# A gated-attention layer's projections in K blocks of 4, 5 and 7 tiles instead of 8 and 8

## The chip, the cores and the metric

The kernel runs on one core of a Trainium2 chip. The core's engines work through queues of their own: the matrix engine (PE, with its weight loads PEld), VectorE (DVE), ScalarE (ACT), GpSimd (POOL) and SyncE (SP), which issues nearly all transfers from HBM. PE writes to PSUM banks, from which DVE and ACT read. An instruction waits at the head of its engine's queue until what it needs is there, and everything behind it waits too. The metric is the device time of one execution in microseconds; the median of several executions is given.

## The reference

A trunk of two layers on 256 tokens of width 2048, all in float32. Layer 0 mixes tokens by gated linear attention (GLA), layer 1 by forgetting attention (FoX); each is followed by a gated MLP with a short convolution. Every sub-layer gets a normalised and modulated input, and the modulation comes from a vector c through a large matrix.

```python
cond = jax.nn.silu(c)
for i in range(DEPTH):
    mod = (cond @ w_mod[i] + b_mod[i])[:, None, :]
    sh_m, sc_m, g_m, sh_f, sc_f, g_f = jnp.split(mod, 6, axis=-1)
    h = rmsnorm(x, norm_mix[i]) * (1.0 + sc_m) + sh_m
    ...
    x = x + (1.0 + g_m) * y          # y: GLA or FoX of h
    h = rmsnorm(x, norm_ffn[i]) * (1.0 + sc_f) + sh_f
    x = x + (1.0 + g_f) * conv_ffn(h, ...)

def gla_mixer(h, w_in, w_gate, b_gate, g_norm, w_out):
    q, k, v, r, a = jnp.split(h @ w_in, ...)   # 1024, 1024, 2048, 2048, 16 columns
    log_alpha = log_sigmoid(a @ w_gate + b_gate) / 16
    ...
```

Only the first part of layer 0 is touched: the columns of sh_m and sc_m (2048 each, a sum over 2048 rows of w_mod), h, and the product h @ w_in.

## The kernel before, in words

Every product is done in three passes, since PE rounds its operands: an operand is split into a rounded part and the rest, and high times high, low times high and high times low are added in PSUM. For the weights, ACT casts a tile of 128 rows by 1024 columns (wh, L120) and DVE subtracts (wl, L124). For the input, `make_h` (L498) works tile by tile of K: DVE multiplies x by the inverse root (hn, L517), ACT applies scale and shift with rounding (h, L518), DVE does it again without rounding (L519) and subtracts (L520). In PE's rows L602 is high times high, L603 the input's low part, L604 the weight's low part; L638 to L640 are the same for v, where h is the moving operand's partner; L652 to L654 the narrow product a. In the changed kernel these lines are L615 to L617, L651 to L653 (v) and L665 to L667 (narrow), the splits L125 and L129, and make_h is L527 (DVE), L528 (ACT), L530 or L532 (new, on ACT) and L533 (DVE).

The projection h @ w_in is cut into seven pieces: q, k, v0, v1, r0, r1 (1024 columns each) and a (16). `gla` (L686) runs them in K blocks: q, k, v0 on K tiles 0 to 3, the same three on tiles 4 to 7, then a, v1, r0, r1 on tiles 0 to 7; `gla_rest` (L732) runs all on tiles 8 to 15. The reason for blocks is that h of a K tile needs its 128 columns of sc_m and sh_m, and these sums take time. `fold` (L702) takes a finished piece out of its four banks: the first part by ACT (L713), later ones by additions on DVE (L715).

The modulation columns come in two ways. The first 512 of each are summed on PE (`early_sum`, L1246: c times 4 tiles of w_mod; then a copy on ACT, L1252, and four narrow products, L1255). The others are accumulated on DVE in the background (`mod_tasks`, L266 and L268, one 128-row tile at a time; then a 32x32 transpose, L278, a reduction, L279, and one product with a constant, L295, before DVE adds the bias, L311). Before, sc_m of tiles 4 to 7 went that way and sh_m of tiles 4 to 7 on PE, in `finish_late` (L1286).

The order of the work is set by the order in which the program is written, with small priorities, and the queues keep it. `tick` (L356), called behind each K tile of a piece, takes a step of the background list when a pace counter is full; `set_pace` spreads the list over so many ticks, and `drain_bg` empties it. The last three tiles of a piece are held and run bank by bank (TAIL), so that banks come free one after another; they have no tick. `split_to` (L561) keeps the splits three tiles ahead of PE and the loads up to six ahead of the splits. The gate's chain in `gla_rest` (products with w_gate L745, log-sigmoid on ACT and DVE L680 to L683, cumulative products L764) is a second list, paced by pace["side"].

Of the kernel before, what the change touches and what calls it, by code (L numbers as in the profile page):

```python
# [13 lines left out]
AF = mybir.ActivationFunctionType  # L14
# [21 lines left out]
SLOAD = 12  # L36
BACK = 1
STAGE = 3
FREE = 0
PEND = 3  # L40
BLOCKS = (8, 8)
HEAD = 4
HEADED = ('q', 'k', 'v0')
# [10 lines left out]
GP0 = 0.7  # L54
# [3 lines left out]
N0, N5 = 4, 5  # L58
BG0, BG1 = 0.95, 0.45
# [13 lines left out]
def kernel(  # L73
# [20 lines left out]
    order = {"v": None, "t": None}  # L94
# [20 lines left out]
    def split_w(src, moving, after=None):  # L115
# [4 lines left out]
        nc.scalar.copy(out=hi, in_=src)  # L120
# [71 lines left out]
    nc.vector.tensor_scalar_mul(vec[:, r0["qn"]:r0["qn"] + 1], vec[:, r0["qn"]:r0["qn"] + 1], float(P) ** -0.5)  # L192
# [5 lines left out]
    def load_bmod():  # L198
        for hh in range(2):
            br = ringt([P, P], "brow")  # L200
            nc.scalar.dma_start(out=br[:96, :], in_=b_mod[hh].rearrange("(r p) -> r p", p=P))
            pb = misc()
            nc.tensor.transpose(pb[:, :96], br[:96, :], ident[:96, :96])
            nc.vector.tensor_copy(out=bm[:, hh * 96:(hh + 1) * 96], in_=pb[:, :96])
# [28 lines left out]
    startup = {"loads": [], "left": SLOAD}  # L233

    def after_startup(on=True):
        es = ExitStack()
        if on and startup["left"] > 0 and len(startup["loads"]) >= BACK:
            startup["left"] -= 1
            es.enter_context(tc.issue_after(startup["loads"][-BACK]))
        return es  # L240

    def mod_tasks(l, key, f0=0, fn=D, wide=False, defer=False, turn=False):
# [8 lines left out]
        def chunk(c0, kt, st):  # L251
            def load():
                st[kt] = bigt([P, per, width], "wm") if wide else ringt([P, per, width], "wm")
                src = w_mod[l, kt * P:(kt + per) * P, s * D + c0:s * D + c0 + width]
                with after_startup():
                    nc.sync.dma_start(out=st[kt], in_=src.rearrange("(k p) m -> p k m", p=P))
# [99 lines left out]
    def tick():  # L356
        prefetch(PEND)
        flush_resting()
        with ExitStack() as es:
# [3 lines left out]
            steps()  # L363

# [133 lines left out]
    def make_h(l, kind):  # L498
# [12 lines left out]
        def make(m):  # L511
# [7 lines left out]
            nc.vector.tensor_scalar(out=t, in0=t, scalar1=sc, scalar2=sh, op0=ALU.mult, op1=ALU.add)  # L519
# [31 lines left out]
    def next_w(kt, cols, hold=None):  # L551
# [4 lines left out]
        if i < STAGE:  # L556
            run, look = min(run, STAGE - i), 1
        split_to(min(i + 1 + run, len(plan)), look)
        return splits.popleft()

    def split_to(end, look=LOOK):  # L561
        while fetched["split"] < end:
            while fetched["load"] < min(fetched["split"] + look, len(plan)):
# [4 lines left out]
                for c0, cn in cols_:  # L568
                    if nk_ == 1:
                        with after_startup():  # L570
                            nc.sync.dma_start(out=wt[:, o:o + cn], in_=w_[kt_ * P:(kt_ + 1) * P, c0:c0 + cn])
                        o += cn
                    else:
                        nc.sync.dma_start(out=wt[:, :nk_ * cn].rearrange("p (k r) -> p k r", r=cn),
                                          in_=w_[kt_ * P:(kt_ + nk_) * P, c0:c0 + cn]
                                          .rearrange("(k p) r -> p k r", p=P))
# [109 lines left out]
    def gla(l, h, finish_late):  # L686
# [35 lines left out]

        run(HEADED, ALL[:HEAD])
        drain_bg()
        finish_late()
        run(HEADED, ALL[HEAD:BLOCKS[0]])
        run([key for key, _ in pieces if key not in HEADED], ALL[:BLOCKS[0]])
        drain_bg()
        kts = ALL[BLOCKS[0]:]
        return kts, pieces, piece, fold, parts  # L730

    def gla_rest(l, kts, pieces, piece, fold, parts):  # L732
# [3 lines left out]
        nc.sync.dma_start(out=wg[RANK:RANK + 1, :], in_=gla_b_gate)  # L736
        fold("a", piece("a", kts, off["a"]))
# [46 lines left out]
        pace["side"], pace["sacc"] = 1.0, 0.0  # L784

        fold("q", piece("q", kts, off["q"]))
# [21 lines left out]
        pace["side"] = 0.5  # L808
        fold("k", piece("k", kts, off["k"]))
# [573 lines left out]
```

## Time and profile before

| | us |
|---|---|
| median of 3 runs (lowest to highest) | 2430.47 (2429.18 to 2430.49) |
| the profiled execution | 2429.0 |
| its span, first to last instruction | 2427.0 |
| PE busy in it | 2384.6 |
| first full-width weight product with low weights (L604) | at 47.02 |
| idle of PE in front of the block boundary's first product (L652, at 192.41) | 1.86 |

The page counts an engine as busy while an instruction of it runs, and PE's count says nothing of the clock: a matmul of 256 columns starts 0.113 us behind the one before it at full clock and 0.213 us at half clock. So the idle rows and the granted clock are read together. All times are from the start of the span.

### The profile page before, as it was taken

Reading aid. Unit: us, or ns where it says so; the run is one execution under the profiler, and the core shown is the slowest. Engines: PE = TensorE matmul, PEld = TensorE weight load, DVE = VectorE, ACT = ScalarE, POOL = GpSimd, SP = SyncE. Lnnn points to the kernel's source line nnn. Section 1 sums busy time; section 2 is a strip of 40 time slices with the busy share of each in tenths; the row PEclk is TensorE's granted clock in tenths of the full one; section 3 lists DMA queues with packets and bytes.
Section 4 is the critical chain, followed back from the end, with each engine's and each line's share of the span. In section 5 each row is a group of like instructions: output and inputs, shape, how many; then the busy total and the mean of one; then the engine's idle time right before and its main releaser. Section 6 shows DMA issues by size and latency. Waiting matters only on the chain.

```text
span 2427.0 us, 46850 instructions
## 1 busy us (share of the span) xinstructions
PE 2384.6 (98%) x19127; PEld 2285.0 (94%) x19131; DVE 1922.6 (79%) x2609; ACT 1252.4 (52%) x1671; POOL 16.2 (1%) x35
## 2 busy tenths in 40 slices
PE   6999999899999999999999999999999999999998
PEld 4898899899999999999988889999999999999998
DVE  4898989888789999986687998877776767777544
ACT  4447454445556665543454455545555555565433
POOL 0000000000000000000000000000000000000000
PEclk9999999999999999999999999999999999999999
DMA  9986968898668988998589887686777777756552
GB/s 376 374 303 222 328 223 312 297 343 293 195 200 297 318 305 311 326 315 314 164 298 314 299 272 251 215 296 228 235 235 228 240 227 236 232 195 217 191 191 104
DMA packets 188148, 638.31 MB, mean 263 GB/s; under 512 B 23705, under 2 KB 24715, under 8 KB 187548
## 3 DMA queue, kind: packets, MB, share of 16 engines
q1 hardware_dynamic: 186968, 634.12, 76.9%
q8 instruction: 149, 2.44, 0.4%
q10 hardware_dynamic: 964, 1.20, 0.1%
q14 instruction: 67, 0.55, 0.1%
HBM read 633.14 MB, written 2.10 MB: 262 GB/s over the span
## 4 chain that ended last, share of the span: by engine, by line
PE 95%; DVE 3%; DMA 1%; ACT 1%; issue 1%; DVEq 0%; SPq 0%
PE pa L604 25%; PE pa L603 25%; PE pa L602 25%; PE pa L640 5%; PE pa L639 5%; PE pa L638 5%; DMA wm<-in_w_mod_dram 1%; DVE wl L124 1%; PE pe L1246 0%; PE pm L473 0%; DVE acc L268 0%; PE pm L846 0%; PE pm L868 0%; PE pm L1057 0%; PE pt L288 0%
## 5 line engine op out<-in xcount | busy, mean ns | idle before, releaser
L120 ACT CAST wh<-w 128x1024 fp32r<-128x1024 f32 x819 | 856.4, 1049 | 1001.8 <-PE pa L603 707.9
L124 DVE TENSOR_TENSOR wl<-w,wh 128x1024 fp32r<-128x1024 f32 x819 | 995.8, 1218 | 408.8 <-ACT wh L120 403.6
L603 PE MATMUL pa<-h,wh 128*128 128x256 f32 x3584 | 990.8, 278 | 3.9 <-DVE h L520 3.9
L602 PE MATMUL pa<-h,wh 128*128 128x256 f32 x3584 | 987.7, 278 | 2.1 <-ACT h L518 2.1
L604 PE MATMUL pa<-h,wl 128*128 128x256 f32 x3584 | 987.3, 278 | 1.2 <-DVE wl L124 1.2
L603 PEld LDWEIGHTS pa<-h,wh 128*128 128x128 f32 x3584 | 675.3, 189 | 5.1 <-DVE h L520 4.9
L602 PEld LDWEIGHTS pa<-h,wh 128*128 128x128 f32 x3584 | 672.3, 188 | 4.9 <-ACT h L518 2.3
L604 PEld LDWEIGHTS pa<-h,wl 128*128 128x128 f32 x3584 | 672.8, 189 | 1.6 <-DVE wl L124 1.5
L603 PE MATMUL pa<-op,wh 128*128 128x256 f32 x1920 | 526.3, 276 | 0.0
L602 PE MATMUL pa<-op,wh 128*128 128x256 f32 x1920 | 526.3, 277 | 0.0
L604 PE MATMUL pa<-op,wl 128*128 128x256 f32 x1920 | 518.5, 276 | 0.3 <-DVE wl L124 0.3
L268 DVE SCALAR_TENSOR_TENSOR acc<-wm,cT,acc 128x1024 f32<-128x1024 f32 (+1 forms) x345 | 433.2, 1256 | 1.0 <-DMA wm<-in_w_mod_dram 0.3
L603 PEld LDWEIGHTS pa<-op,wh 128*128 128x128 f32 x1920 | 360.5, 188 | 0.0
L602 PEld LDWEIGHTS pa<-op,wh 128*128 128x128 f32 x1920 | 360.2, 188 | 0.0
L604 PEld LDWEIGHTS pa<-op,wl 128*128 128x128 f32 x1920 | 355.4, 188 | 0.5 <-DVE wl L124 0.5
L639 PE MATMUL pa<-wh,h 128*128 128x512 f32 x512 | 200.2, 392 | 0.0
L638 PE MATMUL pa<-wh,h 128*128 128x512 f32 x512 | 198.0, 391 | 0.0
L640 PE MATMUL pa<-wl,h 128*128 128x512 f32 x512 | 189.5, 393 | 0.0
L638 PEld LDWEIGHTS pa<-wh,h 128*128 128x128 f32 x512 | 96.1, 188 | 19.4 <-issue 0.2
L640 PEld LDWEIGHTS pa<-wl,h 128*128 128x128 f32 x512 | 95.9, 188 | 19.5
L639 PEld LDWEIGHTS pa<-wh,h 128*128 128x128 f32 x512 | 96.1, 188 | 19.0
L1109 ACT ACTIVATE y<-u,cw 128x256 f32<-128x256 f32 x176 | 101.6, 599 | 6.7 <-DVE act L1125 4.1
(263 smaller groups left out, 1315.0 us busy)
## 6 DMA issues: line engine op xcount, KB each, us to landing
wm<-in_w_mod_dram SPq DMA_DIRECT2D x320, 512.0 KB, 5.2
w<-in_ffn_w_up_dram SPq DMA_DIRECT2D x320, 512.0 KB, 4.5
w<-in_ffn_w_down_dram SPq DMA_DIRECT2D x176, 512.0 KB, 4.4
w<-in_fox_w_in_dram SPq DMA_DIRECT2D x128, 512.0 KB, 5.2
w<-in_gla_w_in_dram SPq DMA_DIRECT2D x96, 512.0 KB, 6.0
wm<-in_w_mod_dram SPq DMA_DIRECT2D x32, 1024.0 KB, 10.7
w<-in_gla_w_out_dram SPq DMA_DIRECT2D x32, 512.0 KB, 5.5
w<-in_ffn_w_up_dram SPq DMA_DIRECT2D x64, 256.0 KB, 4.5
```

What stands on the lines that cost most here:

```text
L120: nc.scalar.copy(out=hi, in_=src)
L124: order["v"] = nc.vector.tensor_tensor(out=lo, in0=src, in1=hi.bitcast(F32), op=ALU.subtract).ins
L268: nc.vector.scalar_tensor_tensor(out=st["a"], in0=wt[:, j, :], scalar=col, in1=st["a"], op0=ALU.mult, op1=ALU.add)
L602: nc.tensor.matmul(o, wh[:, ms], rh, start=(first and m % 2 == 0), stop=False, skip_group_check=True)
L603: nc.tensor.matmul(o, wh[:, ms], rl, start=False, stop=False, skip_group_check=True)
L604: nc.tensor.matmul(o, wl[:, ms], rh, start=False, stop=last, skip_group_check=True)
L638: nc.tensor.matmul(o, lh[:, ts_], wh[:, hs_], start=first, stop=False)
L639: nc.tensor.matmul(o, ll[:, ts_], wh[:, hs_], start=False, stop=False)
L640: nc.tensor.matmul(o, lh[:, ts_], wl[:, hs_], start=False, stop=last)
L1109: nc.scalar.activation(y, u, AF.Identity, scale=cw[:, l * 3 + 2, r:r + 1], bias=cw[:, 6 + l, r:r + 1])
```

## The change

The K blocks become 4, 5 and 7 tiles, and all seven pieces run in each; in the last block a comes second instead of first. The modulation columns of the second and third block are all accumulated on DVE in the background of the block ahead, 640 and 896 columns wide, and finish_late goes away. All pieces have three parts now, so DVE adds two of them. Two hooks empty the background list and ask for the next h at given tile counts. The tokens are loaded ahead of the modulation weights, the turned vectors and biases come behind the token sums, and the loads keep the order in which they are written. In make_h the unrounded operand of K tiles 3 and up is made on ACT. Some paces change.

```diff
-BLOCKS = (8, 8)
+BLOCKS = (4, 5, 7)
-HEADED = ('q', 'k', 'v0')
+STARTS = (0, 4, 9, 16)
+ORDERS = (("q", "k", "v0", "v1", "r0", "r1", "a"),) * 2 + (("q", "a", "k", "v0", "v1", "r0", "r1"),)
...
-GP0 = 0.7
+GP0 = 0.8
...
-N0, N5 = 4, 5
-BG0, BG1 = 0.95, 0.45
+EASE, N5 = 3, 5
+BG0, BG1 = 0.95, 0.75
...
+    def sync_load(out, in_):
+        with ExitStack() as es:
+            if startup["left"] > 0 and startup["last"] is not None:
+                startup["left"] -= 1
+                es.enter_context(tc.issue_after(startup["last"]))
+            startup["last"] = nc.sync.dma_start(out=out, in_=in_).ins
...
+        hooks.pop(fetched["use"], lambda: None)()
...
-            nc.vector.tensor_scalar(out=t, in0=t, scalar1=sc, scalar2=sh, op0=ALU.mult, op1=ALU.add)
+            if m < 3:
+                nc.vector.tensor_scalar(out=t, in0=t, scalar1=sc, scalar2=sh, op0=ALU.mult, op1=ALU.add)
+            else:
+                nc.scalar.activation(t, t, AF.Identity, scale=sc, bias=sh)
...
+        elif i < NEAR:
+            look = 2
...
-        run(HEADED, ALL[:HEAD])
-        drain_bg()
-        finish_late()
-        run(HEADED, ALL[HEAD:BLOCKS[0]])
-        run([key for key, _ in pieces if key not in HEADED], ALL[:BLOCKS[0]])
-        drain_bg()
-        kts = ALL[BLOCKS[0]:]
+        for n_ in range(len(BLOCKS) - 1):
+            run(ORDERS[n_], ALL[STARTS[n_]:STARTS[n_ + 1]])
+        kts = ALL[STARTS[-2]:]
...
+        fold("q", piece("q", kts, off["q"]))
         fold("a", piece("a", kts, off["a"]))
...
-        pace["side"], pace["sacc"] = 1.0, 0.0
-
-        fold("q", piece("q", kts, off["q"]))
+        pace["side"], pace["sacc"] = 1.4, 0.0
+
+        fold("k", piece("k", kts, off["k"]))
         drain_side()
...
-        pace["side"] = 0.5
-        fold("k", piece("k", kts, off["k"]))
+        pace["side"] = 1.0
...
-    for args in todo[:2]:
-        startup["loads"].append(early_load(*args))
     xs = fetch_x()
-    for args in todo[2:WIDE]:
-        startup["loads"].append(early_load(*args))
+    for args in todo[:WIDE]:
+        early_load(*args)
     load_x(xs)
+    with tc.issue_after(order["s"]):
+        turn_rows()
...
-    def finish_late():
-        for j in range(4):
-            early_sum("sh_m", HEAD, j)
-        early_finish("sh_m", HEAD)
-
     def staged_h(m):
-        if m == 0:
-            for j, task in enumerate(mod_tasks(0, "sc_m", HEAD * P, HEAD * P, wide=True)):
-                bg.extend((task, (lambda j=j: early_load("sh_m", HEAD, j), lambda: None)))
-            set_pace(HEAD * len(HEADED) - 3)
-        elif m == HEAD:
+        if m in STARTS[:-2]:
+            n_ = STARTS.index(m) + 1
             for key in ("sc_m", "sh_m"):
-                queue(mod_tasks(0, key, BLOCKS[0] * P, BLOCKS[1] * P, wide=True))
-            set_pace(6 * BLOCKS[0] - HEAD * len(HEADED) - N0)
+                queue(mod_tasks(0, key, STARTS[n_] * P, BLOCKS[n_] * P, wide=True))
+            n_use = 6 * BLOCKS[n_ - 1]
+            set_pace(n_use - EASE)
+            end = fetched["use"] + n_use + (m > 0)
+            hooks[end - 1] = drain_bg
+            hooks[end] = lambda: h(STARTS[n_])
         return first_h(m)
```

In the places below, each row is line, operation, result<-operands and size. Engine ACT at the start, before, and now:

```order
L1252 COPY er_262<-pe_239 128x512
L1252 COPY er_306<-pe_271 128x512
L482 ACT_TABLE_LOAD
L482 ACTIVATE rb_231<-pm_229,epsc 128x256
L120 CAST wh_336<-w_334 128x1024
L120 CAST wh_342<-w_340 128x1024
L518 ACTIVATE h_318<-hn_319,mod 128x256
```

```order
L492 ACT_TABLE_LOAD
L492 ACTIVATE rb_229<-pm_219,epsc 128x256
L1254 COPY er_260<-pe_237 128x512
L1254 COPY er_304<-pe_269 128x512
L125 CAST wh_334<-w_332 128x1024
L125 CAST wh_340<-w_338 128x1024
L528 ACTIVATE h_316<-hn_317,mod 128x256
```

The root of the token mean (rb) now stands ahead of the copies of the modulation sums (er); the casts of two weight tiles stand ahead of the first h in both.

PE at the end of the first four K tiles before (the last row above finish_late is a product of v0), and at the end of block 1 now (the first row is the last product of r1, pm_1149 the narrow piece a, pa_1171 the first bank of q in block 2):

```order
L640 MATMUL pa_661<-wl_665,h_318 128x512
L1246 MATMUL pe_746<-wm_384,cz_123 32x512 x4
L1246 MATMUL pe_746<-wm_446,cz_123 32x512 x4
L1246 MATMUL pe_746<-wm_545,cz_123 32x512 x4
L1246 MATMUL pe_746<-wm_613,cz_123 32x512 x4
L295 MATMUL pm_698<-red_649,quad 128x16
L1255 MATMUL pm_765<-ones,er_763 128x1 x4
L602 MATMUL pa_771<-h_775,wh_682 128x256
```

```order
L617 MATMUL pa_983<-h_316,wl_996 128x256
L302 MATMUL pm_1092<-red_1055,quad 128x20
L665 MATMUL pm_1149<-h_316,wh_1025 128x256
...
L667 MATMUL pm_1149<-h_316,wl_1026 128x256
L615 MATMUL pa_1171<-h_1128,wh_1064 128x256
L615 MATMUL pa_1172<-h_1128,wh_1064 128x256
L615 MATMUL pa_1173<-h_1128,wh_1064 128x256
L615 MATMUL pa_1174<-h_1128,wh_1064 128x256
L616 MATMUL pa_1171<-h_1128,wh_1064 128x256
```

The sums on PE are gone; one product with the constant quad is left, behind the last r1 product and ahead of the narrow piece. ACT at the same place now:

```order
L125 CAST wh_1152<-w_991 128x1024
L528 ACTIVATE h_1128<-hn_1129,mod 128x256
L528 ACTIVATE h_1128<-hn_1134,mod 128x256
L528 ACTIVATE h_1128<-hn_1139,mod 128x256
L726 COPY r_197_1144<-pa_980 128x512
L726 COPY r_197_1144<-pa_981 128x512
L726 COPY r_197_1144<-pa_982 128x512
L726 COPY r_197_1144<-pa_983 128x512
L528 ACTIVATE h_1128<-hn_1211,mod 128x256
L125 CAST wh_1177<-w_993 128x1024
L532 ACTIVATE hn_1129<-hn_1129,mod 128x256
```

The first unrounded operand (L532) stands behind the copies of r1 and a cast.

DVE at the boundary to the last block, before, and now (pa_1929 to pa_1932 are r1's banks):

```order
L124 TENSOR_TENSOR wl_1846<-w_1676,wh_1845 128x1024
L278 STREAM_TRANSPOSE mt_1771<-acc_1328 128x512
L278 STREAM_TRANSPOSE mt_1774<-acc_1328 128x512
L279 TENSOR_REDUCE red_1770<-mt_1771 128x16
L279 TENSOR_REDUCE red_1770<-mt_1774 128x16
L124 TENSOR_TENSOR wl_1876<-w_1708,wh_1875 128x1024
L311 TENSOR_TENSOR mod<-pm_1837,bm 32x8 x4
```

```order
L728 TENSOR_TENSOR r_197_1144<-r_197_1144,pa_1931 128x512
L275 SCALAR_TENSOR_TENSOR acc_1671<-wm_1754,cT,acc_1671 128x896
L728 TENSOR_TENSOR r_197_1144<-r_197_1144,pa_1932 128x512
L129 TENSOR_TENSOR wl_2124<-w_1933,wh_2123 128x1024
L275 SCALAR_TENSOR_TENSOR acc_1671<-wm_1826,cT,acc_1671 128x896 x2
L275 SCALAR_TENSOR_TENSOR acc_1671<-wm_1861,cT,acc_1671 128x896 x2
L285 STREAM_TRANSPOSE mt_2028<-acc_1671 128x512
L285 STREAM_TRANSPOSE mt_2031<-acc_1671 128x384
L286 TENSOR_REDUCE red_2027<-mt_2028 128x16
L286 TENSOR_REDUCE red_2027<-mt_2031 128x12
L318 TENSOR_TENSOR mod<-pm_2064,bm 32x7 x4
```

The last four accumulations of the background list now stand behind the last fold of r1 and a split whose buffer r1 frees.

More of the change, by code (lines that the diff above doesn't have):

```diff
@@ L93 @@
     cnt = [0]
-    order = {"v": None, "t": None}
+    order = {"v": None, "f": None}
     def nm(s):
@@ L119, in split_w @@
         lo = split.tile([P, WCOLS], F32R, tag="wl", name=nm("wl"))[:, o2:o2 + n_]
-        nc.scalar.copy(out=hi, in_=src)
+        with ExitStack() as es:
+            if order["f"] is not None:
+                es.enter_context(tc.issue_after(order["f"]))
+                order["f"] = None
+            nc.scalar.copy(out=hi, in_=src)
         with ExitStack() as es:
@@ L196, with turn_rows @@
     bm = const.tile([P, 192], F32, name="bm")
-    def load_bmod():
-        for hh in range(2):
[L200 to L204, printed above, removed]
+    brows = []
+    for hh in range(2):
+        brows.append(ringt([P, P], "brow"))
+        nc.scalar.dma_start(out=brows[hh][:96, :], in_=b_mod[hh].rearrange("(r p) -> r p", p=P))
+    def turn_rows():
+        pv = misc()
+        nc.tensor.transpose(pv[:, :nrows], rows[:nrows, :], ident[:nrows, :nrows])
+        nc.vector.tensor_copy(out=vec[:, :nrows], in_=pv[:, :nrows])
+        nc.vector.tensor_scalar_mul(vec[:, r0["qn"]:r0["qn"] + 1], vec[:, r0["qn"]:r0["qn"] + 1], float(P) ** -0.5)
+        pb = misc()
+        for hh in range(2):
+            nc.tensor.transpose(pb[:, hh * 96:(hh + 1) * 96], brows[hh][:96, :], ident[:96, :96])
+        nc.vector.tensor_copy(out=bm, in_=pb[:, :192])
     R88 = 2 * FT
@@ L232 @@
     fin = {}
[L233 to L240, printed above, removed]
+    startup = {"last": None, "left": SLOAD}
+    def sync_load(out, in_):
+        with ExitStack() as es:
+            if startup["left"] > 0 and startup["last"] is not None:
+                startup["left"] -= 1
+                es.enter_context(tc.issue_after(startup["last"]))
+            startup["last"] = nc.sync.dma_start(out=out, in_=in_).ins
     def mod_tasks(l, key, f0=0, fn=D, wide=False, defer=False, turn=False):
@@ L1251, in early_finish @@
         rows_ = t2("er")
-        nc.scalar.copy(out=rows_, in_=early.pop((key, f0)))
+        order["f"] = nc.scalar.copy(out=rows_, in_=early.pop((key, f0))).ins
         pt = misc()
@@ L1274 @@
         if i + WIDE < len(todo):
-            startup["loads"].append(early_load(*todo[i + WIDE]))
-        summed = early_sum(*args)
+            early_load(*todo[i + WIDE])
+        with tc.issue_after(order["s"]):
+            summed = early_sum(*args)
         if args[2] == 3:
```

42 lines of the change are left out of this document (14 added, 28 removed).

## The prediction

> **What bounds the kernel now.** I read the page first, then busy time by windows, then the chain of waits, and last the rows of single engines around each place where the matrix engine (PE) stands still. The page's first part says who sets the time:
>
> ```profile
> PE 2384.6 (98%) x19127; PEld 2285.0 (94%) x19131; DVE 1922.6 (79%) x2609; ACT 1252.4 (52%) x1671; POOL 16.2 (1%) x35
> ```
>
> No matmul of a weight stream is added or removed here, so the change can only move the time in which PE stands still or runs slowly. In windows (length, then busy time and count of PE, PE loads, DVE, ACT and POOL, the granted clock, the DMA engines' share, GB/s):
>
> ```profile
> 31.00:51.00 20.00, 13.54 (x78) 11.38 (x77) 15.06 (x31) 14.27 (x24) 0.00 (x0) 0.74 1.04 396
> 51.00:80.00 29.00, 29.00 (x212) 27.23 (x211) 24.94 (x32) 15.63 (x20) 0.00 (x0) 1.00 1.03 390
> 80.00:89.00 9.00, 7.56 (x55) 4.15 (x55) 6.12 (x16) 5.25 (x10) 0.00 (x0) 0.94 0.77 239
> 181.00:195.00 14.00, 11.69 (x97) 11.37 (x96) 13.26 (x24) 7.88 (x13) 0.23 (x2) 0.96 0.65 200
> 226.00:280.00 54.00, 54.00 (x412) 48.92 (x411) 53.90 (x68) 28.03 (x51) 0.64 (x3) 1.00 0.91 310
> ```
>
> The places are the start, the stretch of finish_late (80 to 89, PE "busy" with small sums) and the boundary of the K blocks (181 to 195). Between them PE is full, even where VectorE (DVE) is too (53.90 of 54 us).
>
> **The start gains.** The chain of waits, and below it SyncE's waits and two of its issues:
>
> ```profile
> 37.31 0.96 ACT er L1252 x2
> ...
> 39.59 0.48 ACT rb L482
> ...
> 43.01 0.61 ACT h L518
> ...
> 47.02 0.58 PE pa L604
> ```
>
> ```profile
> SPq L571 <- DMA wm<-in_w_mod_dram: 4.7, 2, 2.4
> SPq L256 <- DMA w<-in_gla_w_in_dram: 2.5, 2, 1.7
> ```
>
> ```profile
> 31.29 0.33 SPq L571 DMA_DIRECT2D w<-in_gla_w_in_dram  x1
> 34.57 0.38 SPq L256 DMA_DIRECT2D wm<-in_w_mod_dram  x1
> ```
>
> Before, root (rb) and sum copies (er) end at 40.1, because tokens land between modulation weights. With tokens first, both chains but the last sum are over early. The bytes ahead of the first weight tiles are the same in both kernels, so I keep the landings: the second issue that waits for modulation weights goes at 31.29 (the last early one is in), the first of L256, which waits for a weight tile, at 34.57 (two tiles of 0.52 MB at 396 GB/s later, so the second tile is in). From 31.3: four sums on PE at a cold clock 1.0, copy er 0.6, four small products 1.0, two vector operations 0.3: the columns stand at 34.25. But on ACT two casts stand ahead of h, the second of the tile landing at 34.57: 35.6. Then h (0.6), and on DVE the rows 37 to 43 of its order, the third h among them, and wl: first L617 at 39.6, where L604 stood at 47.02. **−7.4 us**; −9.1 if the clock is already up then, −5.5 if the cast or DVE is 2 us later.
>
> **finish_late goes.** PE's rows, and the clock behind them:
>
> ```profile
> 80.58 3.64 PE L1246 MATMUL pe<-wm,cz 128*32 128x512 f32 x32
> 84.16 0.40 PE L295 MATMUL pm<-red,quad 128*128 128x16 f32 x2
> 84.93 1.05 PE L1255 MATMUL pm<-ones,er 128*128 128x1 f32 x8 [0.38 <-ACT er L1252]
> 86.87 0.74 PE L602 MATMUL pa<-h,wh 128*128 128x256 f32 x4 [0.89 <-ACT h L518]
> ...
> 88.25 0.42 PE L602 MATMUL pa<-h,wh 128*128 128x256 f32 x1
> ```
>
> ```profile
> 194.00:196.00 2.00, 2.00 (x10) 2.00 (x11) 2.00 (x8) 1.20 (x2) 0.00 (x0) 0.50 0.76 231
> 196.00:198.00 2.00, 2.00 (x15) 2.00 (x14) 2.00 (x7) 1.20 (x2) 0.00 (x0) 0.71 0.05 18
> ...
> 88.00:90.00 2.00, 2.00 (x11) 2.00 (x11) 2.00 (x8) 0.29 (x1) 0.00 (x0) 0.50 1.01 410
> 90.00:92.00 2.00, 2.00 (x13) 2.00 (x13) 1.04 (x4) 0.10 (x1) 0.00 (x0) 0.66 1.02 420
> ```
>
> From 80.58 to 88.25 PE does six stream matmuls, 0.113 us each at full clock: 7.0 lost. Then the half clock until 91.4 (0.66 is the mean of a part at 0.5 and a part at 1), 3.1 us: 1.5 lost. **−8.5**; −7.0 if the clock is cold there anyway.
>
> **The boundary before.** It pays too:
>
> ```profile
> 190.13 0.28 PE L604 MATMUL pa<-h,wl 128*128 128x256 f32 x1
> 190.25 0.30 PE L295 MATMUL pm<-red,quad 128*128 128x32 f32 x2
> 192.41 0.38 PE L652 MATMUL pm<-h,wh 128*128 128x256 f32 x1 [1.86 <-ACT h L518]
> ...
> 194.32 0.42 PE L652 MATMUL pm<-h,wh 128*128 128x256 f32 x1
> ```
>
> Six stream matmuls between 190.47 and 194.32 lose 3.15, the half clock until 197.1 another 1.4: 4.55. This is given back, and two new boundaries are paid. Their prices come from these rows:
>
> ```profile
> 188.57 1.79 ACT L713 COPY r<-pa 128x512 f32<-128x512 f32 x3
> ```
>
> ```profile
> 86.22 2.07 ACT L518 ACTIVATE h<-hn,mod 128x256 fp32r<-128x256 f32 x4 [1.34 <-DVE mod L1259]
> ```
>
> ```profile
> 187.12 1.30 DVE L278 STREAM_TRANSPOSE mt<-acc 128x512 f32<-128x512 f32 x2
> 188.34 1.24 DVE L279 TENSOR_REDUCE red<-mt 128x16 f32<-128x512 f32 x2
> 189.49 1.22 DVE L124 TENSOR_TENSOR wl<-w,wh 128x1024 fp32r<-128x1024 f32 x1
> 190.74 0.69 DVE L311 TENSOR_TENSOR mod<-pm,bm 32x8 f32<-32x8 f32 x4
> ```
>
> ```profile
> L268 DVE SCALAR_TENSOR_TENSOR acc<-wm,cT,acc 128x1024 f32<-128x1024 f32 x60 | 76.7, 1279 | 0.7 <-DMA wm<-in_w_mod_dram 0.3
> L268 DVE SCALAR_TENSOR_TENSOR acc<-wm,cT,acc 128x512 f32<-128x512 f32 x15 | 11.2, 747 | 0.2
> ```
>
> So in a queue one h costs 0.5, an accumulator copy 0.6, mt and red 0.62 each, a cast and a wl about 1, an accumulation of 896 columns 1.15 less 0.08 overlap, 1.07.
>
> **Boundary 1 to 2** (T1 is the last r1 matmul). The quad product L302 stands behind it on PE, four vector additions behind that: columns at T1+1.1. ACT's order is three h, four copies of r1, the fourth h, a cast, and only then L532, which makes the unrounded operand: 1.1 + 1.5 + 2.4 + 0.5 + 0.95 + 0.6 = 7.05. The subtraction on DVE (0.43) releases L616 at T1+7.5. PE has the narrow product a and four matmuls to fill this: 16 × 0.113 = 1.8. Lost 5.7, and 1.4 at half clock: **+7.1** (5.7 if the clock holds; 9 if DVE brings the sums 2 us late). Were L532's work still on DVE, it would not wait behind the copies; the move of the unrounded operand costs here.
>
> **Boundary 2 to 3.** DVE's order after T2 holds the last fold of r1 (0.6), a wl whose cast needs a buffer that r1 frees (1.15), four accumulations (4.3), mt and red of 896 columns (2.25): 8.35. Then L302 (0.5), the additions (0.7): 9.55. ACT: four h (2.05), L532 (0.55), DVE 0.43: L616 of q at T2+12.6. Behind L302 are queued the narrow a and q's first matmuls, 19 × 0.113 = 2.15 of cover. Lost 10.45; DVE's rows of block 2 (126 to 206 of its order, by these durations) sum to some 74 us of PE's 83, so at T2 it may lag by up to the 1.6 us that one fold and an accumulation make; I take half, 0.8. Half clock 1.4: 12.65, less the 4.55: **+8.1** (5.9 to 9.9).
>
> **The gate chain.** From the first gate product to the last cumulative product:
>
> ```profile
> 204.64 1.98 PE L745 MATMUL pm<-wg,aT 17*128 17x512 f32 x4
> ```
>
> ```profile
> 222.72 1.23 DVE L683 SCALAR_TENSOR_TENSOR la<-la,le 128x1024 f32<-128x1024 f32 x1
> ```
>
> ```profile
> 224.00 0.71 PE L764 MATMUL pm<-mgla,la 128*128 128x128 f32 x4 [0.34 <-DVE la L683]
> ```
>
> 19.4 us, which PE covers but for 0.34 to 0.5. With the side work paced 1.4 instead of 1.0, PE's order has only 16.8 us of products between these two places, and the chain, its casts and table loads as before, is some 19.1: 2.3 lost, 1.8 more than before. A standstill of that length, 1.86 and 0.45, sent the clock to 0.50 at 194; so 1.4 more: **+3.2** (0 if fewer casts lie in the chain). [...]
>
> Hidden: the added folds (36 become 48 vector additions) and the accumulations of block 1, about 58 us of DVE in 67, beside a full PE, as in 226 to 280. The row and bias transposes move behind the token sums, where PE waits for weights. If this cover is gone, the third rival has its price. On SyncE's queue the same loads stand in another order, and GpSimd's has none. Later stages differ by L532 alone: nothing, ±1.
>
> **Sum.** −7.4 − 8.5 + 7.1 + 8.1 + 3.2 = +2.5. The profiled execution took 2429.0 (span 2427.0 and 2.0 around it), 1.5 below the median of the runs, 2430.47 (2429.18 to 2430.49). So 2431.5 in its terms, **2433.0** in the runs'.
>
> **Rivals.** *The clock holds and the gate is covered* (faster): fills keep PE warm through the start, and the boundaries lose their bare 5.7 and 5.9. −9.1 − 8.5 + 5.7 + 5.9 + 0 = −6.0: 2424.5. For it: the start has fifteen fill matmuls shortly ahead. Against: 0.50 behind a gap of 2 us. *The load stream sets T1* (slower): PE starts 7.4 earlier on a stream already at a DMA share of 1.03 and 390 GB/s. Behind 31.3 us come 24 tiles of 0.52 MB, 16 modulation tiles of 0.66 and six tiles ahead, 26.2 MB: 67 us at that rate, 98.4, and the last product is due three tiles before T1 (105.7 − 8.2 = 97.5). It decides as soon as the rate falls under 385: DVE waits for a tile, wl behind it, PE behind wl. With a tenth less, 6 us: 2439. Against: in 51 to 80 PE never waited on that stream. *DVE sets block 3* (slower): it holds 7 instead of 8 tiles for six pieces, 16.3 us less of PE, and DVE loses only 6.8 of splits. If the 53.90 of 54 us has no reserve, the difference of 9.5 comes on top: 2442.5. Against: PE lost nothing there.
>
> **How the numbers follow.** Forecast 0.43 (its own range 2427 to 2438), clock held 0.23, load stream 0.21, DVE 0.13. A difference under 0.2% (4.9 us) can't be told from none in this kernel. The first rival gives faster, with little of the forecast's lower end: 0.24. The two slow rivals and the forecast's upper end give slower: 0.36. Same 0.40. Range 2423 to 2442: it takes in the low bounds of all terms (2424.5) and the high ones (−5.5 − 7.0 + 9 + 9.9 + 3.2 = +9.6, 2440).
>
> **What would show it.** The first L617 near 39.6; no L1246-like stretch after it; after the last r1 of blocks 1 and 2 a standstill of PE of about 5.7 and 10 to 11 us, ended by DVE's h (L533), with L532 the last on ACT; a clock near 0.5 for 3 us behind each; a wait of L774 for la near 2 us. It is wrong if these standstills are half as long, if PE waits for wl or DMA inside block 1 or 2, or if the first weight product is not before 42.

## The result and the profile after

The changed kernel takes 2451.71 us (median of 4 runs, 2449.59 to 2453.06), the one before 2430.48 (4 runs, 2429.18 to 2430.52). The ratio is 1.0088, interval 1.0070 to 1.0105: slower by 21 us. The forecast was 2433.0 with a range of 2423 to 2442, so it was wrong. One execution of a kernel below (g1_comb) took 3020 us at a granted clock of 0.746; it is not counted, and fast executions are compared with fast ones.

One sentence of the description of the kernel before has to be corrected: the last three tiles are held and run bank by bank only in the second half of a product that ends in a residual (the output projections and the MLP), not in the seven pieces of the first projection.

The profiled execution took 2453.06 us, its span 2451.3, which is 24.3 more than before. The page's first part:

```profile
PE 2388.0 (97%) x19089; PEld 2292.3 (94%) x19093; DVE 1928.8 (79%) x2596; ACT 1279.2 (52%) x1723; POOL 16.1 (1%) x35
```

The engines' sums are near those of before (3 us more on PE, 6 on DVE, 27 on ACT). The loss is not in work; it is in PE standing still or at half clock, and it has to be looked for by place. Windows around the places (from:to, length, then busy time and count of PE, PE loads, DVE, ACT, POOL, the granted clock, the DMA engines' share, GB/s), of the changed kernel:

```profile
105.00:120.00 15.00, 10.35 (x72) 9.63 (x71) 10.86 (x23) 10.13 (x17) 0.00 (x0) 0.85 0.91 336
200.00:216.00 16.00, 4.31 (x25) 4.12 (x24) 13.35 (x20) 2.76 (x5) 0.23 (x2) 0.63 0.29 79
...
615.00:622.00 7.00, 5.05 (x36) 4.65 (x36) 3.58 (x6) 7.00 (x14) 0.00 (x0) 0.90 0.53 162
```

```profile
244.00:300.00 56.00, 54.55 (x308) 45.54 (x309) 51.08 (x61) 41.81 (x64) 0.23 (x2) 1.00 0.85 290
300.00:366.00 66.00, 66.00 (x610) 63.32 (x609) 56.27 (x84) 32.27 (x49) 3.05 (x8) 1.00 0.80 269
366.00:410.00 44.00, 33.19 (x240) 31.82 (x239) 41.88 (x62) 19.11 (x37) 0.00 (x0) 0.83 0.78 268
```

The first two rows are the two new block boundaries, which the forecast had. The last row of the second fence is one that it had not: from 366 to 410 runs the output projection of GLA, and PE does 240 instructions in 44 us. Before, PE was full there, 470 in 53 us (the first 4.5 us of the row are the end of r1; the output projection's first matmul starts at 361.50):

```profile
357.00:410.00 53.00, 53.00 (x470) 53.00 (x469) 50.58 (x59) 25.62 (x32) 0.00 (x0) 1.00 0.86 304
```

The row of 300 to 366 matters as much: there, in the last block, PE is full at full clock and DVE is busy for 56.27 of 66 us. The damage does not show where the change is made; it shows behind it. PE's waits in the changed kernel (engine, tile and line, what it waited for: us in total, times, the longest):

```profile
PE pm L302 <- DVE red L286: 11.7, 1, 11.7
PE pa L616 <- DVE h L533: 7.7, 4, 3.6
PE pa L615 <- DVE r L728: 3.7, 1, 3.7
PE pa L616 <- DVE op L549: 3.6, 2, 2.9
PE pa L615 <- ACT op L548: 3.5, 2, 2.9
...
PE pm L774 <- DVE la L696: 1.2, 1, 1.2
```

Setting the starts of the same matmuls side by side in both traces, place by place, gives this account (plus is slower):

| place | forecast | measured |
|---|---|---|
| start, to the first L617 | −7.4 | −4.9 |
| finish_late | −8.5 | −8.5 |
| boundary 1 to 2 | +7.1 | +8.2 |
| boundary 2 to 3, less the old boundary | +8.1 | +9.6 |
| gate chain | +3.2 | +1.6 |
| output projection of GLA | 0 | **+18.3** |
| start of the first MLP | 0 | −4.8 |
| MLP, second half of K (617) | 0 | +3.6 |
| sum | +2.5 | about +23.1 |

From about 643 us on the two traces run side by side. Of the 1.2 us between this sum and the 24.3 of the spans, 0.8 lie right behind the first L617: the half clock lasts 5.0 us there (to 47.18), where before it lasted 3.4 behind the first L604 (to 50.39). So 4.1 of the start's 4.9 us reach the stream at full clock. The rest is not placed. Why the MLP's start loses less was not followed up either; PE waited there 3.9 us for ss and 2.0 for h before, and waits 2.9 for h now.

**The start.** PE's rows (start, duration, engine and line, output and inputs, tile, count, in brackets the idle time ahead and what ended it):

```profile
32.46 1.07 PE L1248 MATMUL pe<-wm,cz 128*32 128x512 f32 x8
33.46 1.25 PE L1286 MATMUL pw<-fill 128*128 128x512 bf16 x5
34.64 1.06 PE L1248 MATMUL pe<-wm,cz 128*32 128x512 f32 x8
...
42.16 0.58 PE L617 MATMUL pa<-h,wl 128*128 128x256 f32 x1 [1.71 <-DVE wl L129]
```

The last early weights were there at 31.23, as forecast. But PE was not: it had the sums of the tiles before, and the fill products (L1286) that stand between them, still ahead. The last sum runs at 34.64 and not at 31.3; a part of the 3.3 us is made up on ACT.

**Boundary 1 to 2.** PE's rows, and then ACT's at the same time:

```profile
112.46 0.86 PE L615 MATMUL pa<-h,wh 128*128 128x256 f32 x2 [0.94 <-ACT r L726]
116.94 0.58 PE L616 MATMUL pa<-h,wh 128*128 128x256 f32 x1 [3.62 <-DVE h L533]
```

```profile
111.85 2.02 ACT L726 COPY r<-pa 128x512 f32<-128x512 f32 x4
113.75 0.61 ACT L528 ACTIVATE h<-hn,mod 128x256 fp32r<-128x256 f32 x1
114.25 1.04 ACT L125 CAST wh<-w 128x1024 fp32r<-128x1024 f32 x1
115.18 2.08 ACT L532 ACTIVATE hn<-hn,mod 128x256 f32<-128x256 f32 x4
```

L532, the unrounded operand that was moved to ACT, is last in ACT's queue: behind four copies of r1, an h and a cast. PE needs its result for L616 and has nothing else.

**Boundary 2 to 3.** The last stream matmul of r1 (L617, starting at 200.94) ends near 201.2. DVE's rows from there on:

```profile
201.32 1.87 DVE L728 TENSOR_TENSOR r<-r,pa 128x512 f32<-128x512 f32 x3
203.12 1.14 DVE L275 SCALAR_TENSOR_TENSOR acc<-wm,cT,acc 128x896 f32<-128x896 f32 x1
204.18 0.67 DVE L728 TENSOR_TENSOR r<-r,pa 128x512 f32<-128x512 f32 x1
204.78 1.21 DVE L129 TENSOR_TENSOR wl<-w,wh 128x1024 fp32r<-128x1024 f32 x1
205.91 4.70 DVE L275 SCALAR_TENSOR_TENSOR acc<-wm,cT,acc 128x896 f32<-128x896 f32 x4
210.65 1.17 DVE L285 STREAM_TRANSPOSE mt<-acc 128x512 f32<-128x512 f32 x2
211.74 1.10 DVE L286 TENSOR_REDUCE red<-mt 128x16 f32<-128x512 f32 x2
```

From the last fold at 204.18 to the end of red at 212.84 it is 8.66, which the forecast had as 8.35 (its terms add to 8.30). Ahead of it lie three folds and an accumulation, 2.9 us, where the forecast allowed 0.8.

**The output projection.** PE's second large standstill there:

```profile
402.16 1.22 PE L615 MATMUL pa<-op,wh 128*128 128x256 f32 x4 [2.89 <-ACT op L548]
406.26 0.58 PE L616 MATMUL pa<-op,wh 128*128 128x256 f32 x1 [2.87 <-DVE op L549]
```

Its operand op is made from the normalised heads of GLA. The normalisation of heads 2 and 3 needs an inverse root, which DVE works out in thirteen instructions (the function rsqrt, lines 398 to 416), each of which needs the one ahead of it. They work on 128 x 4 elements and take 0.16 us each. The side list gives the whole chain to the program at once, but the scheduled order on DVE spreads it out among the large instructions. DVE's rows, first the arrival of the sums that it needs, then a piece of it, then its end:

```profile
362.35 0.15 DVE L894 COPY pvar<-pm 128x2 f32<-128x2 f32 x1
...
382.36 0.16 DVE L410 TENSOR_TENSOR rt<-rv,grs 128x4 f32<-128x4 f32 x1
382.46 1.22 DVE L129 TENSOR_TENSOR wl<-w,wh 128x1024 fp32r<-128x1024 f32 x1
383.61 1.28 DVE L275 SCALAR_TENSOR_TENSOR acc<-wm,cT,acc 128x1024 f32<-128x1024 f32 x1
384.80 0.15 DVE L411 TENSOR_TENSOR rt<-rt,grs 128x4 f32<-128x4 f32 x1
...
390.99 0.48 DVE L422 TENSOR_SCALAR dg<-ident,grs 128x128 f32<-128x128 f32 x2
...
397.12 1.21 DVE L905 TENSOR_TENSOR oT<-oT,pm 128x1024 f32<-128x1024 f32 x1
...
400.78 1.28 DVE L922 TENSOR_TENSOR oT<-oT,th 128x512 f32<-128x512 f32 x2
```

Thirteen instructions of 0.16 us, 2.1 us of work, take 28.6 us from pvar to dg. The multiplication by the root (L905) and the gate (L922) follow in the same queue, and the cast to op that PE waits for comes behind them. The same chain before, its first and last row, and then PE's first matmul of the output projection:

```profile
334.49 0.16 DVE L885 COPY pvar<-pm 128x2 f32<-128x2 f32 x1 [0.64 <-PE pm L884]
...
358.49 0.48 DVE L412 TENSOR_SCALAR dg<-ident,grs 128x128 f32<-128x128 f32 x2
```

```profile
361.50 0.28 PE L602 MATMUL pa<-op,wh 128*128 128x256 f32 x1
```

That was slow too: 24.0 us. But it began 27.0 us before the output projection's first matmul and ended 3.0 us before it; now it begins 5.4 us before that matmul (367.74) and ends 23 us behind it. The chain thus ends 26 us later against the projection, 21.6 by its later begin and 4.6 by its longer way. Counted in weight tiles of PE's order from the start of the output projection, the diagonal products of heads 2 and 3 stood at tiles −0.1 to 2.7 before and stand at 6.3 to 8.0 now, and the projection needs heads 2 and 3 from tile 8 on. The third block has seven tiles instead of eight for six pieces, so everything that is paced beside it (scores, application, sums) has come nearer to the end.

### The profile page after: what moved, and what is told of

Same layout as the page of the kernel before. It is cut to its first block, busy times and chain, and to the rows that moved or that the text cites. A ratio compares the mean times of both kernels' runs of the same rounds, so it can differ in the third digit from the quotient of the medians.

```text
span 2451.3 us, 46838 instructions
## 1 busy us (share of the span) xinstructions
PE 2388.0 (97%) x19089; PEld 2292.3 (94%) x19093; DVE 1928.8 (79%) x2596; ACT 1279.2 (52%) x1723; POOL 16.1 (1%) x35
## 4 chain that ended last, share of the span: by engine, by line
PE 90%; DVE 5%; DMA 2%; ACT 1%; issue 1%; SPq 0%; DVEq 0%; ACTq 0%
PE pa L617 24%; PE pa L616 24%; PE pa L615 24%; PE pa L652 4%; PE pa L653 4%; PE pa L651 4%; DVE wl L129 1%; DVE acc L275 1%; DMA wm<-in_w_mod_dram 1%; DMA w<-in_gla_w_in_dram 1%; PE pe L1248 0%; PE pm L483 0%; ACT wh L125 0%; PE pm L855 0%; DMA xtok<-in_x_dram 0%
## 5 line engine op out<-in xcount | busy, mean ns | idle before, releaser
L616 PE MATMUL pa<-h,wh 128*128 128x256 f32 x3584 | 993.1, 278 | 9.4 <-DVE h L533 9.4
L617 PE MATMUL pa<-h,wl 128*128 128x256 f32 x3584 | 989.1, 278 | 1.7 <-DVE wl L129 1.7
L616 PEld LDWEIGHTS pa<-h,wh 128*128 128x128 f32 x3584 | 677.0, 189 | 11.6 <-DVE h L533 10.5
L617 PEld LDWEIGHTS pa<-h,wl 128*128 128x128 f32 x3584 | 674.2, 189 | 2.8 <-DVE wl L129 1.9
L616 PE MATMUL pa<-op,wh 128*128 128x256 f32 x1920 | 530.8, 278 | 3.6 <-DVE op L549 3.6
L617 PE MATMUL pa<-op,wl 128*128 128x256 f32 x1920 | 526.2, 277 | 0.0
L275 DVE SCALAR_TENSOR_TENSOR acc<-wm,cT,acc 128x1024 f32<-128x1024 f32 (+2 forms) x360 | 444.5, 1235 | 11.9 <-DMA wm<-in_w_mod_dram 10.7
L616 PEld LDWEIGHTS pa<-op,wh 128*128 128x128 f32 x1920 | 363.2, 189 | 4.1 <-DVE op L549 4.1
L617 PEld LDWEIGHTS pa<-op,wl 128*128 128x128 f32 x1920 | 360.4, 189 | 0.0
```

Of the source, the lines that this page charges most:

```text
L275: nc.vector.scalar_tensor_tensor(out=st["a"], in0=wt[:, j, :], scalar=col, in1=st["a"], op0=ALU.mult, op1=ALU.add)
L616: nc.tensor.matmul(o, wh[:, ms], rl, start=False, stop=False, skip_group_check=True)
L617: nc.tensor.matmul(o, wl[:, ms], rh, start=False, stop=last, skip_group_check=True)
```

## The experiments

Two theories were set against each other. **Theory 1:** each loss has its own local cause, an instruction late in an in-order queue. It is L532 at boundary 1, accumulations behind the block's end at boundary 2, and the inverse-root chain at the output projection, late because block 3 is a tile shorter. **Theory 2:** there is a general shortage (of DVE's time or of the load stream) in the first 450 us, so that what is saved at one place comes back at the next.

Most kernels here ran once, and the four runs of the changed kernel spread by 3.5 us: a difference of that size between two times says nothing by itself. The losses of single places are read from the traces.

**x5_nonorm: heads 2 and 3 without their normalisation.** Their scale and their two normalisations are left out; they go into the output projection unnormalised, and the output differs.

```diff
-        side.extend((apply(2), apply(3), scale_of(0), scale_of(2), normalise(0), normalise(1), normalise(2), normalise(3)))
+        side.extend((apply(2), apply(3), scale_of(0), normalise(0), normalise(1)))
```

> The changed kernel with one thing left out: the output of heads 2 and 3 of the gated attention is not multiplied by its inverse root (the factors and the multiplication of heads 2 and 3 are gone), so the output differs. Theory 1, the chain of small steps behind the last block (scores, apply, inverse roots, factors) is late, and the output projection waits for it at its ninth K tile: the wait of 2.9 + 2.9 us at 399 to 406 us and the half clock behind it go, 6 to 8 us; 2443 to 2446. Theory 2, VectorE is simply full with splits and accumulations there: the operands of tile 9 come as late as before, the wait stays within 2 us; 2449 to 2452.

2440.66 us (one run; the kernel before on the same chip 2430.71, median of 13), 2 below the range of theory 1. The window of the output projection in this kernel, columns as above:

```profile
366.00:410.00 44.00, 40.86 (x327) 39.73 (x326) 43.27 (x49) 22.99 (x42) 0.00 (x0) 0.92 0.83 276
```

327 instructions instead of 240. The loss falls from 18.3 to 7.2, and the standstills at 402 and 406 are gone. So the normalisation of heads 2 and 3, the chain and the multiplications behind it together, costs 11 us. This run does not part the late begin of the chain from its slow way through the queue. What is left is the first standstill (wait for r, 3.7 in the changed kernel), which comes from the folds and gates of r that are late in DVE's queue too.

**e2_dve: the unrounded operand back on DVE, for all tiles.**

```diff
-            if m < 3:
+            if m < 99:
                 nc.vector.tensor_scalar(out=t, in0=t, scalar1=sc, scalar2=sh, op0=ALU.mult, op1=ALU.add)
```

> The changed kernel with the unrounded operand back on VectorE for all tiles. Theory 1, on ScalarE it stands behind the copies of r1 and casts: the wait at the first boundary falls from 7 us to about 3, and the wait of 2.0 us with 1.6 at half clock at the second half of the MLP's K (617 us) goes; together 6 to 8 us; 2443 to 2446. Theory 2, VectorE is the bottleneck of these blocks, and what it takes back (0.33 us for each of 13 tiles) makes the second boundary and the output projection later by as much: 2449 to 2454.

2438.64 us (one run, beside the same 2430.71): 13 faster than the changed kernel, twice what was expected. Boundary 1 in this kernel:

```profile
105.00:120.00 15.00, 13.78 (x114) 13.07 (x114) 14.05 (x31) 9.62 (x15) 0.00 (x0) 1.00 0.90 330
```

114 instructions in the window instead of 72, clock 1.00 instead of 0.85: the loss there falls from 8.2 to 2.3 (the window ends at 120, before the changed kernel's half clock does). Boundary 2 stays at 13.9, since DVE and not ACT ends the wait there. The rest comes from places that were not part of the expectation: the loss at 617 goes (4.2 to 0.6; PE waits for L533 there as well), the MLP's start gives about 2, the gate and the output projection about 1 each. Within the changed kernel the move to ACT thus costs 13 us, for the reason that theory 1 gives: ACT has room on average (52% busy), but not at the places where PE waits.

**e5_448: blocks of 4, 4 and 8 tiles.**

```diff
-BLOCKS = (4, 5, 7)
+BLOCKS = (4, 4, 8)
-STARTS = (0, 4, 9, 16)
+STARTS = (0, 4, 8, 16)
```

> The changed kernel with blocks of 4, 4, 8 tiles: the last block as long as before. Theory 1, a last block of 7 tiles gives the side work (scores, apply, roots) five tiles less of matrix work to hide behind: with 8 tiles the loss at the output projection (18 us in the changed kernel, 366 to 410 us) falls to 8 or less; the second boundary grows by 4 to 6 us, since eight accumulations of 1024 columns stand there instead of five of 896; 2442 to 2448. Theory 2, the length of the block is not what makes it late (VectorE's load per tile is the same): the loss stays 15 to 19 us and with the longer boundary the total is 2455 to 2460.

2449.24 us (one run, before 2431.07, median of 7), 1 above the range of theory 1. The output projection's window, and then what DVE does at boundary 2 in this kernel:

```profile
366.00:410.00 44.00, 41.87 (x354) 41.67 (x353) 44.00 (x60) 21.88 (x30) 0.00 (x0) 0.96 0.85 279
```

```profile
195.41 10.51 DVE L275 SCALAR_TENSOR_TENSOR acc<-wm,cT,acc 128x1024 f32<-128x1024 f32 x8
```

The output projection's loss falls from 18.3 to 4.2: with eight tiles in the last block the chain is nearly in time. It begins at 362.15, 16.8 us before the projection's first matmul (378.96), and takes 24.6 us; the missing tile is thus about half of the 21.6 us by which it began later in the changed kernel, and the rest stays open. This happens although DVE is busy for 44.00 of 44 us there, more than in the changed kernel (41.88). So it is the place of the chain and not a lack of DVE time that costs. (The longer standstill at boundary 2 ahead of it differs as well; what that alone does to the chain was not tried.) Nearly 13 of the 14 us are lost again at boundary 2, where block 2 has a tile less to hide the accumulations, and they are 1024 columns wide instead of 896: eight of them stand in a row behind the block's end, PE waits 21.6 us for red, and the loss grows from 14.1 to some 25, with 1.7 more ahead of it in block 2. The expectation had only 4 to 6 us for that; the place was right, the size was not.

**b2_bg: background work moved from the last block's first part to its second.**

```diff
-BG0, BG1 = 0.95, 0.75
+BG0, BG1 = 0.4, 0.95
```

> The changed kernel with the background accumulations of the last block thinned from 0.95 to 0.4 a tile, and 0.95 instead of 0.75 from r0 on. Theory 1, VectorE's load in the last block delays the chain: the applies come some 3 tiles earlier in the queue, the first wait of the output projection (7 us at 367) goes and the second (11 us at 399) shrinks; 2441 to 2446. Theory 2, the chain's lateness comes from the place of its pieces, not from the load: both waits stay, or the second grows by the denser accumulations; 2450 to 2455.

2462.66 us (one run, before 2431.07), 11 slower than the changed kernel. The first wait in the output projection shrinks (loss before the second one 7.2 to 1.7), but PE now waits 9.1 us for dg itself, and the MLP's start gets worse by the accumulations that were put off (waits of 6.0 for ss, 0.95 and 0.67 for wl; a loss near 16 in place of 5). The time lies beyond both expectations. The chain begins earlier here, 14.8 us before the projection's first matmul (352.35 to 367.18), but takes 47.3 us to dg (399.67): an early begin alone is not enough. The result goes with theory 2 as far as the accumulations are concerned: they were put off and then stood in the way at the MLP's start. Since the second pace was raised at the same time, it doesn't tell what the first alone would do for the chain.

**e7_afirst: a first in the last block, as before the change.** The gate's chain then has q beside it at the old pace, and k follows.

```diff
-... + (("q", "a", "k", "v0", "v1", "r0", "r1"),)
+... + (("a", "q", "k", "v0", "v1", "r0", "r1"),)
...
-        fold("q", piece("q", kts, off["q"]))
         fold("a", piece("a", kts, off["a"]))
...
-        pace["side"], pace["sacc"] = 1.4, 0.0
+        pace["side"], pace["sacc"] = 1.0, 0.0
...
-        fold("k", piece("k", kts, off["k"]))
+        fold("q", piece("q", kts, off["q"]))
         drain_side()
...
-        pace["side"] = 1.0
+        pace["side"] = 0.5
+        fold("k", piece("k", kts, off["k"]))
```

> The changed kernel with the narrow piece a first in the last block and the side paces of before (1.0 beside q, then 0.5). Theory 1, the gate chain is earlier, but what follows waits for k and for VectorE: the waits for the gate (2 us at 243 and 262) go, the loss at the output projection stays 14 to 20 us; 2447 to 2453. Theory 2, the place of a is what made the chain late: the loss at the output projection falls under 8 us; 2438 to 2443.

2454.95 us (one run, before 2431.07), 2 above the range of theory 1. The gate's wait of 1.2 is down to 0.3, but a wait of 1.9 for wl near 292 has come, and the output projection loses some 18 to 19, as before, with this wait in it:

```profile
PE pm L424 <- DVE dg L422: 8.5, 1, 8.5
```

The chain begins 7.2 us before the projection, about as in the changed kernel. The order and pace of the first half of the last block are thus not what makes it late.

**e3_keep: without the fill products at the start.**

```diff
-KEEP = 5
+KEEP = 0
```

> The changed kernel without the 15 fill matmuls between the early sums. Theory 1, at the start the matrix engine's own queue is late: the last early weights landed at 31.2 us, but their sums began at 34.6 behind sums and fills of 0.21 us each. Without fills (3.2 us) the first product with low weights comes at 39 instead of 42.2; 2448 to 2450 beside the change's 2452. Theory 2, the fills keep the clock up: without them the sums and first products are slower, and the first product comes at 42 or later; 2451 to 2454.

2450.45 us (one run, before 2430.71). The time is within the changed kernel's own runs; the trace tells more. The last early sum runs at 32.66 instead of 34.64 and the first L617 at 40.36 instead of 42.16: 1.8 us gained at that place. The fills explain about 1.8 of the 2.5 us by which the forecast of the start was off. The rest is not PE's queue in this run: the last sum stands 1.07 us waiting for its weights, which land some 1.4 us later than in the changed kernel's trace.

**s1_tok: tokens first alone, in the kernel before.** The diff is cut to its core.

```diff
-    for args in todo[:2]:
-        startup["loads"].append(early_load(*args))
     xs = fetch_x()
-    for args in todo[2:WIDE]:
+    for args in todo[:WIDE]:
         startup["loads"].append(early_load(*args))
     load_x(xs)
+    with tc.issue_after(order["s"]):
+        turn_rows()
```

> The kernel before with one part of the change: tokens loaded first, early sums, vectors and biases behind the token sums. Blocks, folds and finish_late as before. Theory 1, the start's gain of 4.9 us stands by itself: first product with low weights at 42.2 instead of 47.0, and all later stages move by as much; 2425.0 to 2426.5, ratio 0.998. Theory 2, it is given back where loads come last (finish_late's weights, or the boundary at 190 us): 2429 to 2431.

2431.35 us (10 runs, 2428.54 to 2431.59) beside 2430.71 (13 runs): ratio 1.000, interval 0.999 to 1.001. The start gains 4.9 us, as in the changed kernel. When the clock is full again 3.6 of it are left (the half clock lasts 6.2 us behind the first low-weight product, 3.4 before), behind finish_late 1.3, since PE waits 2.64 us for h there instead of 0.89, and behind the K boundary the kernel is 1.6 us later than the one before. DVE's rows at that boundary in this kernel:

```profile
190.01 0.65 DVE L282 TENSOR_REDUCE red<-mt 128x16 f32<-128x512 f32 x1
190.58 1.21 DVE L124 TENSOR_TENSOR wl<-w,wh 128x1024 fp32r<-128x1024 f32 x1
191.71 0.68 DVE L282 TENSOR_REDUCE red<-mt 128x16 f32<-128x512 f32 x1
```

A wl stands between the two reductions, and PE waits 3.08 us for the second. So theory 2's time came, but not by the load stream that it named: it is one in-order queue again. The early start was worth nothing here, since the next place that PE waits at did not come earlier with it.

**g1_comb: the changed kernel with four mendings together.** These are e2_dve, e3_keep, a first in the last block with a side pace of 1.0 throughout, and BG0, BG1 = 0.4, 0.75.

> Four edits on the changed kernel together: unrounded operand on VectorE, no fill matmuls, a first with side pace 1.0, background at 0.4 and 0.75 a tile. If their effects add: 12 us from the operand (measured), 1 from the fills (measured), the first wait at the output projection (7 us) and the gate's 2: 2428 to 2432, beside 2430.5 before. If the second wait goes too, 2420 to 2424. If VectorE's load only moves to the output projection and the MLP's start, 2434 to 2440.

2448.5 us (three runs, 2448.45 to 2449.38; before 2431.07), ratio 1.0074, interval 1.0054 to 1.0094. That is over the whole range of the expectation, and slower than e2_dve alone. The first part of the output projection still loses 10.4, and the stretch from 440 to 500 us, its end and the start of the MLP, some 20 (9.9 before, about 5 in the changed kernel), with a wait of 5.5 for ss in it. The chain begins 23.2 us before the projection, nearly as early as before the change, and takes 41.3 us. So what is taken from one standstill turned up at the next, as theory 2 says, but this run does not show that it had to: b2_bg, which thins the background in the same way at first, was 11 us slower and e7_afirst 3, e2_dve 13 faster and e3_keep 1, and these four add up to nothing too.

**u10 and t10_best: the old blocks, with the background work done earlier.** Both keep blocks of 8 and 8 tiles. In u10 one number is changed in the kernel before: the background list of the first block is to be empty ten instead of four ticks ahead of its end (a tick is one K tile of one piece). t10_best has tokens first (as s1_tok) and no fills as well.

```diff
-N0, N5 = 4, 5
+N0, N5 = 10, 5
```

> The kernel before with blocks of 8 and 8, tokens loaded first, no fill matmuls at the start, and the background accumulations of the first block spread to end 10 instead of 4 ticks early. Theory 1: in the run with tokens first alone the start's gain was lost where a reduction stood behind a split on VectorE's queue at the block boundary; with the sums early in that queue the boundary's 4.5 us go and the start keeps 5 to 7: 2418 to 2422. Theory 2: what the start gains is lost again in finish_late or at another place of the first block: 2425 to 2430.

> The kernel before with one number changed: the background accumulations of the first block end 10 instead of 4 ticks early. Theory 1: the boundary's wait at 190 us (3.1 and 1.4 at half clock) goes and nothing else changes: 2425.5 to 2427. Theory 2: the earlier accumulations delay the splits of the first block, on a load stream that is full there: 2429 to 2433.

| | us, median of 5 (range) | before, same chip | ratio (interval) |
|---|---|---|---|
| t10_best | 2419.87 (2419.14 to 2420.87) | 2429.96 | 0.9957 (0.9943 to 0.9971) |
| u10 | 2418.89 (2418.29 to 2422.03) | 2429.96 | 0.9956 (0.9944 to 0.9969) |

Two windows of u10, the old K boundary and the start of the MLP:

```profile
181.00:195.00 14.00, 13.89 (x122) 13.70 (x121) 9.92 (x23) 8.08 (x15) 0.23 (x2) 1.00 0.62 195
445.00:475.00 30.00, 27.09 (x221) 25.43 (x220) 26.14 (x51) 16.78 (x25) 0.00 (x0) 1.00 0.66 206
```

At the boundary PE now does 122 instructions where it did 97, at full clock: the loss of 4.5 is down to 0.5. The start of the MLP loses 3.9 instead of 9.9. Together these are 10.0 of the 11.1 us. The boundary is what was expected; the other 6 us, by which the kernel is below its whole expectation, were not. At 445 PE waits 2.3 us for ss instead of 3.9, and the clock stays at 1.00, where before it was 0.50 from 453.2 to 460.0. How an earlier end of the first block's background brings this about stays open. Tokens first adds nothing to it (the two intervals are the same). Both beat the kernel before and the changed one.

## Why the prediction was wrong, by its own steps

**The step that failed is "Later stages differ by L532 alone: nothing, ±1."** It holds three of the eight places in the account, +18.3, −4.8 and +3.6, together +17 of the 20 us between forecast and measurement. A part of this was in reach of the trace before. The inverse-root chain took 24.0 us there and ended at 358.49, 3.0 us before the output projection's first matmul, and the block beside it was to lose a tile for six pieces; how much later the chain would then end was not counted. The forecast looked at DVE's share in the last block and asked whether there was enough of it. The share was enough (56.27 of 66 us); the position wasn't. Shown by x5_nonorm (without the normalisation of heads 2 and 3, −11) and e5_448 (with eight tiles, −14 at this place). The +3.6 is L532's own: it goes in e2_dve, so "L532 alone" was mis-sized as well.

**The third rival named the right condition and the wrong mechanism.** "Block 3 holds 7 instead of 8 tiles for six pieces" is the condition of the largest loss, as e5_448 shows. But it was argued with DVE as a bound inside the block, at 9.5 us, and there PE lost nothing to it (66.00 of 66 us busy at full clock). What it costs is paid behind the block and is 14 to 18 us. The range ended at the rival's 2442.5 and left out that more than one bad case could hold.

**The start: right in kind, mis-sized.** −4.9 instead of −7.4. The landings were right, the step "From 31.3: four sums on PE" was not: PE's own queue was 3.3 us behind. e3_keep shows the fills in 1.8 of the 2.5 us that the first L617 came late. The forecast's own marker, wrong if the first weight product is not before 42, fell at 42.16.

**finish_late: right**, −8.5, and no wait of PE in block 1, so the rival on the load stream fell too.

**Boundary 1: right, with its mechanism.** +8.2 for a forecast of 7.1; L532 was the last on ACT, as was said, and e2_dve shows 5.9 of it to be the move of the unrounded operand.

**Boundary 2: right in its mechanism, 1.5 too small.** DVE was 2.9 us behind at the block's end, and 0.8 had been taken. At both boundaries the half clock was sized too small: it ends at 122.27 and 217.85, 5.3 and 5.0 us behind the first product after the standstill (116.94 and 212.90), and costs about 2.6 and 2.5, where the prediction took 1.4 from the old boundary.

**The gate: right in place, twice too large.** The waits are 0.34 and 1.2 us, where 2.3 were forecast, and the half clock of 1.4 didn't come (1.00 in the window of 244 to 300). Whether a wait of 2.3 us would have cost the clock there was not shown.

**The first rival** (clock held, gate covered) fell: the clock is 0.85 and 0.63 at the two boundaries.

## What to carry to other kernels

When a stage is made shorter, list what is paced beside it and runs out behind it, and for each such chain compare its end with the moment at which it is needed; the chain here, whose begin moved 21.6 us nearer to that moment, came late, though DVE was busy for only 56.27 of 66 us ahead of it. The tiny dependent instructions of that chain, in a full in-order queue, took the time of the large ones between them, not their own (28.6 us for 2.1 us of work). Before work is moved to the less busy engine, look at what stands ahead of it in that engine's queue at the few places where the matrix engine waits; and try first to end the background work earlier, which here took one number and gave 11 us, more than half of them at a place where they were not looked for.

## What the runs showed that was not expected

**Small instructions, large delay.** Thirteen instructions of 0.16 us took 24.0 us before and 28.6 after, about 2 us for each link, which is one wl (1.2) or an accumulation (1.28) and a little more. In b2_bg they took 47.3.

**How short a wait costs the clock.** A single wait of 1.2 us (L774) left it at 1.00, and so did 1.0 and 0.2 at boundary 1 of e2_dve. Two waits of 0.89 and 1.06 did not. PE's rows of the changed kernel:

```profile
618.61 0.38 PE L615 MATMUL pa<-h,wh 128*128 128x256 f32 x1 [0.89 <-ACT u L1140]
620.05 0.38 PE L616 MATMUL pa<-h,wh 128*128 128x256 f32 x1 [1.06 <-DVE h L533]
620.28 0.28 PE L617 MATMUL pa<-h,wl 128*128 128x256 f32 x1
...
620.81 0.42 PE L616 MATMUL pa<-h,wh 128*128 128x256 f32 x1
```

The matmuls behind the second wait still run at full clock (0.28 us), and some 0.6 us later they fall to half (0.42). The granted clock by windows:

```profile
617.00:620.50 3.50, 1.55 (x11) 1.15 (x10) 0.86 (x3) 3.50 (x8) 0.00 (x0) 1.00 0.58 176
621.00:624.00 3.00, 3.00 (x16) 3.00 (x15) 2.68 (x7) 3.00 (x7) 0.00 (x0) 0.50 0.22 33
624.50:627.00 2.50, 2.50 (x25) 2.50 (x24) 1.61 (x3) 2.50 (x5) 0.00 (x0) 1.00 0.31 125
```

PE is idle for 1.95 us of the first window, the second runs at 0.50, and the third is at 1.00 again. At the old boundary the two waits were 1.86 and 0.45, with 0.50 in the window of 194 to 196. A single wait of 1.97 us, longer than any of these four, that ends at 471.70 in the trace before left the clock at 1.00 (windows of 468 to 472 and 472 to 476), and so did the 2.3 us for ss in u10 (445 to 475). So the length of the longest single wait does not part these cases; what does was not shown.
